# A hybrid diffusion step on one core: modulation sums queued singly behind VectorE sums of FF1, and 28 unread matmuls at the seam into FF1

## The chip, the cores and the metric

The kernel runs on one core of one Trainium2 chip. Its engines run side by side, each with a queue of its own: PE multiplies matrices into PSUM banks, VectorE (DVE) and ScalarE (ACT) do elementwise work and read the banks out, GpSimd (POOL) does a little elementwise work, and SyncE (SP) issues nearly all transfers. The metric is the device time in microseconds (us) of one execution; the median of three runs counts.

## What is computed

One inference step of one layer: a normalisation with a modulation, one input projection, a Fourier mixer and a windowed attention as two branches, a gated merge, an output projection with a residual, then a second modulated normalisation and a squared-ReLU MLP, and a last normalisation. There are 1024 latent tokens and 128 context tokens, 1024 channels wide; the MLP is 4096 wide. Cut to what matters here:

```
def modulation(cvec, w_ada, b_ada):
    m = jax.nn.silu(cvec) @ w_ada + b_ada
    return [t[:, None, :] for t in jnp.split(m, 6, axis=-1)]    # sh1, sc1, ga1, sh2, sc2, ga2

def channel_mixer(h, w_ff1, w_ff2):
    return jnp.square(jax.nn.relu(h @ w_ff1)) @ w_ff2

    x = x + ga1 * merge_branches(u_f, attn_o, g, w_fo, w_ao, w_out)
    h = rmsnorm(x, g2) * (1 + sc2) + sh2
    x = x + ga2 * channel_mixer(h, w_ff1, w_ff2)
```

The modulation vectors of both token kinds are six chunks of 1024 columns of one product with w_ada. The last, ga2, is wanted only when the MLP's result is added.

## The kernel before

**Arithmetic.** Every 32-bit operand is split into a rounded high part and the rest, the low part: ScalarE copies the high part (L145), VectorE subtracts it from the raw one (`sub`, L140). A product is three matmuls: high by high, high by low, low by high. Such a split is what stands between a weight's landing and its first use on PE; the low part is used by the third matmul.

**Stages.** Input projection, Fourier mixer, attention, branch projections, output projection (`wout_mm`, token tiles in three groups), FF1 and FF2. FF1 and FF2 work by a seven-product scheme (Strassen's) on blocks of tokens and channels. FF1 goes over 16 column pairs of w_ff1 (256 columns each). The body of a pair `p` takes seven products with 512 columns of tokens (`prod`, L1267: 12 matmuls each) and one product for the context tokens (`step_ctx`, L1311: 24 matmuls with 256 columns). The products go into PSUM banks from a pool of six (`gt`); the small ones, transposes among them, into a pool of two (`mmt`). VectorE adds banks up (`ev_p6`, `ev_p7`, `ev_c2`, `ev_p3`: L1341, L1350, L1355, L1367), ScalarE applies the squared ReLU (L1286, L1287), VectorE forms block sums for FF2's scheme (L1380 to L1389), and SP stores the blocks. VectorE also forms weight sums for the next products (`ff1_sums`, L1089 to L1092, one of which goes into the tile `SA`, which was the context tile's place before).

**The modulation's steps.** From the third chunk on the modulation is worked off in blocks of 256 columns, beside other work (`mod_blocks`, L286). A block is ten steps. Steps 0 to 7 each load 128 x 256 of w_ada over SP (L299) into one of two slots and do two VectorE operations with it, one for each token kind (L310 in step 0, L312 in the others), which add a multiple of it to an accumulator. Steps 8 and 9 transpose and sum up (L321, L322). `mod_fold`, called in the middle of the next block, ends a block with a small matmul and four additions (L268, L272). 40 steps (`MOD_LATE`), the four blocks of ga2, are left when FF1 begins. In FF1 the two slots and the accumulator lie in `zh(15, 2)`, the place of the last tile of the output projection (L1493).

**Who sets the order.** The code is traced in the order of its lines, and a planner that simulates the engines puts each engine's instructions into a queue: an instruction that is ready in its simulation may be drawn ahead of others that were traced earlier, and the earlier traced goes first among those that are ready. Between L1239 and L1492, the seam from the output projection into FF1, the order of PE, VectorE, ScalarE and GpSimd is written out by hand: `manual_schedule` keeps the listed instructions in their order, but instructions traced after it can still be put between them. `tc.issue_after(ins)` lets what is traced under it be queued on the engine of `ins` only behind `ins`; instructions on other engines, a load on SP for example, are not bound by it.

**The seam.** In this order PE does: the last parts of the output projection (`unit_end`), products 1 and 2 of the first pair with three of four token tiles (`step_p1(0, RA)`, which needs one of the six banks free; `step_p2`, which adds into the same bank after ScalarE has read it in `ev_p1`, L1296), products 6, 7, 5, 4, 3 with transposes (`fin_c`, L1165) between, then the same products for the last token tile (`RB`), the context tile's transposes, the context product and its last transposes. The context product needs `cth` and `ctl`, the high and low parts of the context tile: a ScalarE copy (L1481) and a VectorE subtraction (L1482, recorded as L140, BT<-ZR). After it the loop over pairs 1 to 15 begins (L1541).

Of the kernel before, what the change touches and what calls it, by code (L numbers as in the profile page):

```python
# [14 lines left out]
ALU = mybir.AluOpType  # L15
# [22 lines left out]
CH = 384  # L38
# [20 lines left out]
def backbone_kernel(  # L59
# [26 lines left out]
    nc = tc.nc  # L86
    uid = [0]

    def nm(s):
        uid[0] += 1  # L90
        return f"{s}_{uid[0]}"
# [32 lines left out]
    def mmt():  # L124
        return pmm.tile([P, 512], F32, tag="mm", name=nm("mm"))
# [43 lines left out]
    def mod(k, m, tok):  # L169
        return mods[:, k * 8 + m, tok : tok + 1]  # L170
# [161 lines left out]
    def mod_step(n):  # L332
        for _ in range(n):
            if msteps:
                msteps.pop(0)()

    with ExitStack() as sf:
        qa = sf.enter_context(tc.tile_pool(name="qa", bufs=6, space=PSUM))

        def bank6():  # L340
            return qa.tile([P, 512], F32, tag="x", name=nm("x"))
# [4 lines left out]
        with ExitStack() as s0:  # L346
# [6 lines left out]
            ps = mmt()  # L353
# [29 lines left out]
            for t0 in range(0, NTT, 3):  # L383
# [8 lines left out]
                for t, xt in zip(range(t0, t0 + 3), xts):  # L392
# [4 lines left out]
                    for hh in range(2):  # L397
                        ps = bank6()
# [102 lines left out]
        for o in range(0, NDFT, 1024):  # L501
            n = min(1024, NDFT - o)
# [9 lines left out]
        for gi in range(4):  # L512
# [17 lines left out]
            for s in range(4):  # L530
                r = slice(s * 512, (s + 1) * 512)
                anchor = mm3(pa, sth[:, s], stl[:, s], dhi[:, r], dlo[:, r], s == 0, s == 3)
            for s in range(2):
                r = slice(2048 + s * 256, 2304 + s * 256)
# [22 lines left out]
            e = gi % 2  # L557
# [371 lines left out]
    def gt():  # L929
        return q3.tile([P, 512], F32, tag="x", name=nm("x"))  # L930
# [27 lines left out]
    with ExitStack() as sao:  # L958
# [18 lines left out]
        for m in range(KC):  # L977
# [4 lines left out]
            for j in range(NJ):  # L982
                r = slice(j * CH, (j + 1) * CH)
# [7 lines left out]
        for m in range(KC):  # L991
            blk = load_w(w_ao, 0, KC, m * P, P)
            for j in range(NJ):
                ps = gt()
# [22 lines left out]
    def tsel(n):  # L1017
        return (tev, TE[n]) if n in TE else (tbv, TB[n])
# [61 lines left out]
    def uhi(raw):  # L1080
        h_, l_ = (wp.tile([P, D], F32R, tag=w, name=nm(w), bufs=3) for w in ("whi", "wlo"))
        nc.scalar.copy(h_, raw)
        return h_, l_
# [20 lines left out]
    def wout_mm(ps, t, h, k, w):  # L1104
        c = slice(h * HB, (h + 1) * HB)
        mh, ml = mview(t)[:, 0, k, :], mview(t)[:, 1, k, :]
        wh, wl = w
        nc.tensor.matmul(ps, mh, wh[:, 0, c], start=(k == 0), stop=False)
        nc.tensor.matmul(ps, mh, wl[:, 0, c], start=False, stop=False)
        nc.tensor.matmul(ps, ml, wh[:, 0, c], start=False, stop=(k == KC - 1))  # L1110
# [49 lines left out]
    def fin_c(t, kh):  # L1160
        tok = 0 if t < 8 else 1
        px = mmt()
        hn, yt = XS[t % 3], ys[t]
        for q in range(4):
            nc.tensor.transpose(px[:, q * P : (q + 1) * P], hn[:, (kh * 4 + q) * P : (kh * 4 + q + 1) * P], ident)  # L1165
        for q in range(4):
            k = kh * 4 + q
            src = px[:, q * P : (q + 1) * P]
            if kh == 0:
                nc.scalar.activation(yt[:, k], src, AF.Identity, bias=mod(3, k, tok), scale=s2[:, k, tok : tok + 1])  # L1170
            else:
                nc.vector.tensor_scalar(yt[:, k], src, s2[:, k, tok : tok + 1], mod(3, k, tok), ALU.mult, ALU.add)
# [74 lines left out]
    def unit_end(t, h):  # L1247
        wout_mm(b3[t, h], t, h, *last[1])

    T = {}  # L1250
    for n in (1, 2, 3, 4, 5, 6, 7):
        v, j = tsel(n)
        T[n] = [(v[:, :, j, 0, k, :], v[:, :, j, 1, k, :]) for k in range(4)]

    def wsel(p, i):
        u = wu[p]
        if i in (1, 2, 4):
            h_, l_ = u[1] if i == 1 else u[2]
            c = slice(P, 2 * P) if i == 4 else slice(0, P)
            return [(h_[:, k, c], l_[:, k, c]) for k in range(4)]  # L1260
        h_, l_ = u["u3"] if i in (5, 6) else u["u4"]
        e = {5: 0, 6: 1, 7: 0, 3: 1}[i]
        return [(h_[:, e, k], l_[:, e, k]) for k in range(4)]

    R4 = (0, 4)

    def prod(ps, p, i, r=R4, cont=False):  # L1267
        t0, tn = r
        po = ps[:, : tn * P].rearrange("p (t c) -> p t c", t=tn)
        for k, ((wh, wl), (xh, xl)) in enumerate(zip(wsel(p, i), T[i])):  # L1270
            xh, xl = xh[:, t0 : t0 + tn], xl[:, t0 : t0 + tn]
            nc.tensor.matmul(po, wh, xh, start=(k == 0 and not cont), stop=False, skip_group_check=cont)  # L1272
            nc.tensor.matmul(po, wh, xl, start=False, stop=False, skip_group_check=cont)  # L1273
            nc.tensor.matmul(po, wl, xh, start=False, stop=(k == 3), skip_group_check=cont)  # L1274
# [4 lines left out]
    def win(x, r):  # L1279
        return x[:, : r[1] * P]  # L1280

    def obuf(p, r, what):
        return place[p][what][:, r[0] * P : (r[0] + r[1]) * P]

    def relu2(v):
        nc.scalar.activation(v, v, AF.Relu)  # L1286
        nc.scalar.activation(v, v, AF.Square)  # L1287

    def step_p1(p, r=R4):
        s_ = st[p, r] = {"a": gt()}  # L1290
        prod(s_["a"], p, 1, r)

    def ev_p1(p, r=R4):
        s_ = st[p, r]
        s_["u2"] = obuf(p, r, 0)
        nc.scalar.copy(s_["u2"], win(s_["a"], r))  # L1296

    def step_p2(p, r=R4):
        prod(st[p, r]["a"], p, 2, r, cont=True)
# [38 lines left out]

    def ev_p6(p, r=R4):
        s_ = st[p, r]  # L1340
        nc.vector.tensor_tensor(s_["u2"], win(s_["b"], r), s_["u2"], ALU.add)  # L1341

    def step_p7(p, r=R4):
        st[p, r]["c"] = gt()
# [2 lines left out]
    def ev_p7(p, r=R4):  # L1347
        s_ = st[p, r]
        s_["u3"] = obuf(p, r, 2)
        nc.vector.tensor_tensor(s_["u3"], win(s_["c"], r), s_["u2"], ALU.add)  # L1350

    def ev_c2(p, r, half, keep):
        s_ = st[p, r]
        v = obuf(p, r, 3) if keep else s_["u3"]
        nc.vector.tensor_tensor(v, win(s_["d" if half else "e"], r), s_["u3"], ALU.add)  # L1355
        relu2(v)

    def step_p5(p, r=R4):
        st[p, r]["d"] = gt()
        prod(st[p, r]["d"], p, 5, r)  # L1360
# [50 lines left out]
    u2 = uhi(flat(r1))  # L1411
# [5 lines left out]
    wu[0][2] = tuple(map(k4, u2))  # L1417
    for h in range(2):
        unit_end(8, h)
    step_p1(0, RA)  # L1420
    ev_p1(0, RA)
    step_p2(0, RA)
    fin_b1(6, 2)
    u3 = uhi(zh(9, 2))
# [46 lines left out]
    step_p5(0, RB)  # L1471
    step_p6(0, RB)
    ev_p6(0, RB)
    fin_c(8, 0)
    fin_c(8, 1)
    step_p2(0, RB)
# [54 lines left out]
    def pre_prep():  # L1531
# [6 lines left out]
        load_hc(2, hc_tile("whi"))  # L1538
        load_hc(3, hc_tile("wlo"))

    for p in range(1, NPR):  # L1541
        if p == 1:
            ff1_u(p, 2)
        step_p1(p)
        ev_p1(p)
        step_p4(p)
        if p > 1:
            step_p3(p - 1)
            ev_p3(p - 1)
            del wu[p - 1]  # L1550
        ff1_sums(p)
        step_p2(p)
        ev_p2(p)
        if p + 1 < NPR:
            ff1_load(p + 1)
        else:
            pre_load()
        step_ctx(p)
        step_p6(p)
        ev_p6(p)  # L1560
        store_57(p - 1)
        step_p7(p)
        ev_p7(p)
        store_63(p - 1)
        ev_c2(p, R4, 0, True)
        store_first(p, 1)
        store_first(p, 2)
        if p + 1 < NPR:
            ff1_u(p + 1, 1)
        else:  # L1570
            pre_prep()
        step_p5(p)
        ev_c2(p, R4, 1, False)
        store_first(p, 4)
        if p + 1 < NPR:
            ff1_u(p + 1, 2)
        step_ctx2(p)
        if 1 < p < 15:
            mod_step(3)
        if p == 14:  # L1580
            mod_step(len(msteps))
            mod_fold()
            ga_rows(5, 2)
# [335 lines left out]
```

## Time and profile before

| | us |
|---|---|
| median of three runs | 1704.38 |
| lowest and highest of the three | 1703.29, 1705.64 |
| the profiled execution, its own time | 1706.87 |
| its span in the trace | 1705.1 |
| PE busy in the span | 1637.5 (96%) |
| VectorE busy | 1184.5 (69%) |
| ScalarE busy | 904.3 (53%) |

The span runs from the first to the last instruction; 1.8 us of the execution lie around it. The seam lies between 960 and 1016 us, the rest of FF1 ends near 1340, FF2 at the end of the span. A wait is put down to the one whose signal came last. "PEclk" is the clock that was granted to PE as a share of 2.4 GHz; the lower level, 1.2 GHz, is 0.50, and a value between is a mean over a stretch with both.

### The profile page before, as it was taken

The numbers are of one execution on the slowest core, as the hardware profiler recorded it, in microseconds if no ns is written. First come the engines' busy times: TensorE is split into PE (matmuls) and PEld (weight loads), VectorE is DVE, ScalarE is ACT, GpSimd is POOL, SyncE is SP. The second block draws the span as 40 slices with busy tenths as digits, with TensorE's granted clock in tenths as the row PEclk, the third lists the DMA queues.
The fourth block names the chain that finished last, engine by engine and source line by source line (L and its number), as shares of the span: only waits on it lengthen the run. The fifth ranks groups of instructions, "written<-read, shape, count | busy, mean of one in ns | idle before, by whom it ended". The sixth has DMA issues, their size and how long they took to land.

```text
span 1705.1 us, 26303 instructions
## 1 busy us (share of the span) xinstructions
PE 1637.5 (96%) x9025; PEld 1452.8 (85%) x9025; DVE 1184.5 (69%) x2408; ACT 904.3 (53%) x1826; POOL 296.1 (17%) x374
## 2 busy tenths in 40 slices
PE   6999999999999999999999879999999999999997
PEld 5799889999899999899987778888888888888886
DVE  7553247778778877778757878668666488777764
ACT  6443236766767777656446644544444354444542
POOL 3410004434434544300001500000000200000000
PEclk9999999999999999999999999999999999999999
DMA  8341491223322311279655425544444996566751
GB/s 298 112 137 64 136 245 49 78 76 80 96 69 78 94 58 50 93 243 314 190 197 176 158 87 180 178 148 149 161 143 149 291 386 216 188 195 193 249 163 62
DMA packets 204629, 265.56 MB, mean 156 GB/s; under 512 B 31992, under 2 KB 132280, under 8 KB 204496
## 3 DMA queue, kind: packets, MB, share of 16 engines
q1 hardware_dynamic: 196240, 253.92, 46.3%
q0 software_dynamic: 8256, 9.96, 2.2%
q8 instruction: 71, 1.16, 0.3%
q14 instruction: 62, 0.51, 0.1%
HBM read 195.38 MB, written 68.44 MB: 155 GB/s over the span
## 4 chain that ended last, share of the span: by engine, by line
PE 74%; DVE 8%; DMA 4%; ACT 4%; issue 3%; POOL 2%; SPq 0%; DVEq 0%; ACTq 0%; POOLq 0%
PE x L1661 6%; PE x L1662 6%; PE x L1663 6%; PE x L1272 6%; PE x L1274 6%; PE x L1273 6%; PE mm L193 3%; PE mm L194 3%; PE mm L195 3%; PE x L195 2%; PE x L194 2%; PE x L193 2%; PE ptp L748 2%; DVE pt L707 2%; PE o L759 1%
## 5 line engine op out<-in xcount | busy, mean ns | idle before, releaser
L140 DVE TENSOR_TENSOR wlo<-wraw,whi 128x1024 fp32r<-128x1024 f32 x100 | 125.7, 1260 | 84.2 <-ACT whi L145 84.0
L145 ACT CAST whi<-wraw 128x1024 fp32r<-128x1024 f32 x98 | 102.5, 1050 | 101.8 <-DMA wraw<-in_w_ff_dram 21.5
L1662 PE MATMUL x<-BR 128*128 128x512 f32 x336 | 130.7, 389 | 0.0
L1663 PE MATMUL x<-BR 128*128 128x512 f32 x336 | 130.2, 389 | 0.0
L1661 PE MATMUL x<-BR 128*128 128x512 f32 x336 | 129.0, 389 | 0.0
L729 POOL TENSOR_SCALAR pt<-pt,mx 128x512 f32<-128x512 f32 (+2 forms) x144 | 96.7, 684 | 160.5 <-DVE mx L727 144.1
L719 ACT ACTIVATE pt<-pt,mx 128x513 f32<-128x513 f32 (+2 forms) x144 | 94.7, 660 | 32.7 <-DVE mx L717 32.2
L707 DVE CUSTOM_DVE_ANT_0 pt<-s,mask,sink 128x512 f32<-128x512 f32 (+2 forms) x144 | 94.7, 673 | 21.7 <-PE ptp L748 11.9
L1634 ACT CAST BR<-aa 128x512 fp32r<-128x512 f32 x80 | 49.7, 622 | 103.4 <-PE x L1662 48.2
L140 DVE TENSOR_TENSOR pl<-ptp,ph 128x512 fp32r<-128x512 f32 (+1 forms) x136 | 86.0, 640 | 14.1 <-ACT ph L753 12.8
L305 POOL TENSOR_TENSOR macc<-macc,mprod 128x512 f32<-128x512 f32 x70 | 91.9, 1313 | 20.1 <-ACT mprod L303 20.0
L194 PE MATMUL mm<-BR,whi 128*128 128x384 f32 x272 | 92.5, 340 | 0.0
L753 ACT CAST ph<-ptp 128x512 fp32r<-128x512 f32 (+1 forms) x136 | 72.5, 546 | 32.5 <-PE ptp L748 31.2
L1272 PE MATMUL x<-BR,whi 128*128 128x512 f32 (+2 forms) x204 | 80.0, 392 | 7.4 <-ACT ZR L1296 4.8
L193 PE MATMUL mm<-BR,whi 128*128 128x384 f32 x240 | 83.9, 350 | 0.0
L195 PE MATMUL mm<-BR,wlo 128*128 128x384 f32 x240 | 82.0, 342 | 0.0
L1274 PE MATMUL x<-BR,wlo 128*128 128x512 f32 (+2 forms) x204 | 78.4, 384 | 1.9 <-DVE wlo L140 1.9
L748 PE MATMUL ptp<-ident,pt 128*128 128x128 f32 x496 | 76.1, 275 | 2.2 <-ACT qT L689 2.1
L1273 PE MATMUL x<-BR,whi 128*128 128x512 f32 (+2 forms) x204 | 78.2, 383 | 0.0
L1663 PEld LDWEIGHTS x<-BR 128*128 128x128 f32 x336 | 63.0, 188 | 13.2
L1661 PEld LDWEIGHTS x<-BR 128*128 128x128 f32 x336 | 63.1, 188 | 13.1
L1662 PEld LDWEIGHTS x<-BR 128*128 128x128 f32 x336 | 63.1, 188 | 12.9
(460 smaller groups left out, 5195.0 us busy)
## 6 DMA issues: line engine op xcount, KB each, us to landing
aa<-hr_d SPq DMA_DIRECT2D x108, 256.0 KB
ab<-in_w_ff_dram SPq DMA_DIRECT2D x108, 256.0 KB
hr_d<-ZR SPq DMA_DIRECT2D x104, 256.0 KB
wraw<-in_w_in_dram SPq DMA_DIRECT2D x40, 512.0 KB
wraw<-in_w_ff_dram SPq DMA_DIRECT2D x34, 512.0 KB
mraw<-in_w_ada_dram SPq DMA_DIRECT2D x96, 128.0 KB
wraw<-in_w_out_dram SPq DMA_DIRECT2D x24, 512.0 KB
z_d<-z SPq DMA_DIRECT2D x48, 192.0 KB
```

Source lines behind the costliest of these rows:

```text
L140: eng.tensor_tensor(dst, raw, hi.bitcast(F32), ALU.subtract)
L193: nc.tensor.matmul(out, ah, bh, start=start, stop=False)
L194: nc.tensor.matmul(out, ah, bl, start=False, stop=False)
L195: return nc.tensor.matmul(out, al, bh, start=False, stop=stop).ins
L707: nc.vector.tensor_tensor_reduce(out=pt[:, e, :n], in0=sp[:, :n], in1=mask[:, m0 : m0 + n], scale=1.0, scalar=sink8[:, h0 + e : h0 + e + 1 ...
L748: nc.tensor.transpose(pst[:, bi, e, :], pt[:, e, b * P : (b + 1) * P], ident)
L1272: nc.tensor.matmul(po, wh, xh, start=(k == 0 and not cont), stop=False, skip_group_check=cont)
L1273: nc.tensor.matmul(po, wh, xl, start=False, stop=False, skip_group_check=cont)
L1274: nc.tensor.matmul(po, wl, xh, start=False, stop=(k == 3), skip_group_check=cont)
L1661: nc.tensor.matmul(ps, xh, bh, start=start, stop=False, skip_group_check=cont)
L1662: nc.tensor.matmul(ps, xh, bl, start=False, stop=False, skip_group_check=cont)
L1663: nc.tensor.matmul(ps, xl, bh, start=False, stop=stop, skip_group_check=cont)
```

## The change

Two things are done.

1. `mod_step(3)` at the end of the bodies of pairs 2 to 14 is taken out. Instead, in the bodies of pairs 2 to 11, one step each is traced behind `ev_p6`, `ev_p7` and both `ev_c2`, under `issue_after` of that VectorE sum: four steps a pair, 40 in all. The rest of the work on ga2 (`mod_fold`, `ga_rows`) comes at the end of pair 12, before at pair 14.
2. `unread(n)` issues n matmuls of 128x128 by 128x384 into a small bank that nobody reads, with the high part of the token block `T[1][0]` as both operands. 9 are put behind `unit_end(8, ...)`, 12 behind `ev_p1(0, RA)` and 7 behind `ev_p6(0, RB)`, all within the hand-written order.

```diff
+    def unread(n):
+        ps, (a, b) = mmt(), T[1][0]
+        for _ in range(n):
+            nc.tensor.matmul(ps[:, :CH], a[:, 0], a[:, 0:3], start=True, stop=True)
+
     def ev_p6(p, r=R4):
         s_ = st[p, r]
-        nc.vector.tensor_tensor(s_["u2"], win(s_["b"], r), s_["u2"], ALU.add)
+        return nc.vector.tensor_tensor(s_["u2"], win(s_["b"], r), s_["u2"], ALU.add).ins
...
     for h in range(2):
         unit_end(8, h)
+    unread(9)
     step_p1(0, RA)
     ev_p1(0, RA)
+    unread(12)
     step_p2(0, RA)
...
     step_p6(0, RB)
     ev_p6(0, RB)
+    unread(7)
     fin_c(8, 0)
...
+    def mod_behind(p, ins):
+        if 1 < p < 12:
+            with tc.issue_after(ins):
+                mod_step(1)
+
     for p in range(1, NPR):
...
         step_p6(p)
-        ev_p6(p)
+        mod_behind(p, ev_p6(p))
         store_57(p - 1)
         step_p7(p)
-        ev_p7(p)
+        mod_behind(p, ev_p7(p))
         store_63(p - 1)
-        ev_c2(p, R4, 0, True)
+        mod_behind(p, ev_c2(p, R4, 0, True))
...
         step_p5(p)
-        ev_c2(p, R4, 1, False)
+        mod_behind(p, ev_c2(p, R4, 1, False))
         store_first(p, 4)
...
         step_ctx2(p)
-        if 1 < p < 15:
-            mod_step(3)
-        if p == 14:
+        if p == 12:
             mod_step(len(msteps))
             mod_fold()
             ga_rows(5, 2)
```

`ev_p7` and `ev_c2` return their VectorE sum in the same way.

## Rows read from the trace of the kernel before

**Rows 1.** The page, part 1: busy time, share of the span, instructions.

```profile
PE 1637.5 (96%) x9025; PEld 1452.8 (85%) x9025; DVE 1184.5 (69%) x2408; ACT 904.3 (53%) x1826; POOL 296.1 (17%) x374
```

**Rows 2.** Windows of FF1 and FF2: length; busy (instructions) of PE, PEld, DVE, ACT, POOL; PEclk, DMA, GB/s.

```profile
1016.00:1340.00 324.00, 324.00 (x1614) 274.67 (x1613) 222.67 (x343) 150.34 (x233) 5.80 (x9) 1.00 0.50 158
1340.00:1690.00 350.00, 349.45 (x1543) 288.87 (x1542) 248.87 (x427) 153.58 (x282) 4.37 (x7) 1.00 0.67 224
```

**Rows 3.** Waits of PE from 950 to 1016 us: in total, times, longest.

```profile
PE x L1272 <- ACT ZR L1296: 4.8, 1, 4.8
PE mm L1319 <- DVE BT L140: 4.2, 1, 4.2
PE x L1272 <- DVE ZR L1120: 2.5, 1, 2.5
PE x L1274 <- DVE wlo L140: 1.9, 1, 1.9
PE mm L1165 <- ACT ZR L1153: 1.7, 1, 1.7
```

**Rows 4.** Windows of 4 us over the seam, columns as in rows 2.

```profile
964.00:968.00 4.00, 1.28 (x8) 0.96 (x6) 3.90 (x6) 2.94 (x7) 3.84 (x3) 1.00 0.35 131
968.00:972.00 4.00, 1.87 (x6) 1.87 (x7) 3.56 (x10) 2.77 (x7) 0.41 (x1) 0.56 0.80 253
972.00:976.00 4.00, 4.00 (x16) 4.00 (x15) 3.13 (x4) 3.13 (x5) 0.00 (x0) 0.59 0.63 181
...
1000.00:1004.00 4.00, 0.53 (x2) 0.53 (x3) 3.19 (x7) 0.00 (x0) 0.00 (x0) 0.82 0.26 80
...
1008.00:1012.00 4.00, 3.91 (x22) 3.09 (x21) 2.21 (x6) 3.40 (x5) 0.00 (x0) 0.82 0.38 128
```

**Rows 5.** Timeline at PE's second long wait: start, length, engine, line, what [idle before].

```profile
996.03 1.36 DVE L1172 TENSOR_SCALAR ZR<-mm,s,mods 128x128 f32<-128x128 f32 x4
997.52 1.04 ACT L1481 CAST BT<-ZR 128x1024 fp32r<-128x1024 f32 x1
1000.81 1.28 DVE L312 SCALAR_TENSOR_TENSOR ZR<-ZR,siluc 128x256 f32<-128x256 f32 x3 [0.84 <-DMA ZR<-in_w_ada_dram]
1002.20 1.82 DVE L140 TENSOR_TENSOR BT<-ZR,BT 128x1024 fp32r<-128x1024 f32 x2
1003.47 0.58 PE L1319 MATMUL mm<-whi,BT 128*128 128x256 f32 x1 [4.23 <-DVE BT L140]
```

**Rows 6.** Timeline: a step's load and sum, and the last transposes of two pairs.

```profile
1009.38 0.33 SPq L299 DMA_DIRECT2D ZR<-in_w_ada_dram  x1
1011.55 0.88 DVE L312 SCALAR_TENSOR_TENSOR ZR<-ZR,siluc 128x256 f32<-128x256 f32 x2 [1.28 <-DMA ZR<-in_w_ada_dram]
...
1121.28 0.38 PE L1329 MATMUL mm<-ident,ZR 128*128 128x128 f32 x2
1143.50 0.38 PE L1329 MATMUL mm<-ident,ZR 128*128 128x128 f32 x2
```

**Rows 7.** Timeline of PE: two matmuls at full clock, two in the first dip.

```profile
964.77 0.33 PE L1273 MATMUL x<-BR,whi 128*128 128x384 f32 x1
964.95 0.34 PE L1274 MATMUL x<-BR,wlo 128*128 128x384 f32 x1
...
970.62 0.52 PE L1273 MATMUL x<-BR,whi 128*128 128x384 f32 x1
970.94 0.52 PE L1274 MATMUL x<-BR,wlo 128*128 128x384 f32 x1
```

**Rows 8.** Groups by line, VectorE, 990 to 1330 us: busy, mean ns, idle before.

```profile
L312 DVE SCALAR_TENSOR_TENSOR ZR<-ZR,siluc 128x256 f32<-128x256 f32 x56 | 25.2, 478 | 9.8 <-DMA ZR<-in_w_ada_dram 9.7
```

**Rows 9.** Windows in the attention and in FF1, columns as in rows 2.

```profile
374.00:378.00 4.00, 2.17 (x13) 1.50 (x12) 3.92 (x10) 1.94 (x5) 0.00 (x0) 0.99 0.23 54
...
1032.00:1053.00 21.00, 21.00 (x108) 17.73 (x107) 17.76 (x35) 10.05 (x16) 0.00 (x0) 1.00 0.43 138
...
1116.00:1137.00 21.00, 21.00 (x107) 17.80 (x106) 12.59 (x18) 10.20 (x17) 0.00 (x0) 1.00 0.43 145
```

## What the change does to the time: the prediction

> **What bounds the kernel now.** I read the page first: the matrix engine (PE) is busy for 96% of the span [rows 1]. Next the windows: from 1016 to 1340 us it is busy for all 324 us and from 1340 to 1690 us for 349.45 of 350 [rows 2]. So behind 1016 us, in FF1 and FF2, PE alone sets the pace, and what the stage before it ends earlier, the kernel ends earlier. Third, the waits of PE in the stretch ahead, the seam between the output projection and FF1: 4.8, 4.2, 2.5, 1.9 and 1.7 us [rows 3], 15 us in all, the largest loss near the lines that the change touches. Last, windows of 4 us over the seam, for the clock [rows 4]. In two stretches the granted clock is at its lower level, 1.2 GHz for 2.4. A row's clock gives the length: 0.56 over 4 us is 3.5 us at half, so the first dip begins at 968.5 us, and 0.59 in the next row ends it at 975.3. The second runs from 1002.6 (0.82) to 1009.4 us (0.82). Each begins inside one of the two longest idle times of PE and outlasts it.
>
> **Why PE idles in the second.** The context product needs its token tile's low part (L1482, on VectorE through L140). VectorE is free of the manual order's work at 996.03 + 1.36 = 997.4 us, and the high part is there at 997.52 + 1.04 = 998.6 [rows 5]. But the low part is taken only behind 1002.20 us. Between them stand modulation sums (L310, L312) that the planner drew forward from the second pair's body, and they also wait for their own loads: 0.84 us at 1000.81 [rows 5], and later 1.28 us at 1011.55 [rows 6], with the subtraction behind them for which PE waits 1.9 us [rows 3]. VectorE takes its queue in order here, so a sum whose row block has not landed holds what stands behind it.
>
> **The change, part 1: the sums.** They are neither removed nor added. All 40 steps left for FF1 go from three at the end of a body (pairs 2 to 14) to four in each body of pairs 2 to 11, each behind a sum that reads a PE bank. That pins VectorE's part; the loads on SP are not pinned, but with two slots only two of them can go early. None of the sums can then stand in the seam. What that frees there:
> - The gap of 4.23 us. VectorE would do the two short steps of the manual order that stand ahead (0.68 and 0.28 us) from 997.6 to 998.6, just when the high part is there; the subtraction takes about 1.2 us, so PE resumes near 999.9 in place of 1003.47 [rows 5]: 3.6 us. Lower bound 2.5, if one more 128x512 subtraction (0.7 us) and a handover slip in ahead of it.
> - The second dip. From 1003.47 to 1009.4 us PE works 5.9 us at half. Its matmuls of 384 columns start every 0.32 us in the first dip and every 0.18 us at full clock [rows 7], so 44% of the time is lost: 2.6 us. With a gap of 0.7 us left there I see no dip. Lower bound 1.3, if half of it stays.
> - The wait of 1.9 us at the first pair's low half. Taken off is the load wait of 1.28 us [rows 6]: 1.3 us; between 0 and 1.9.
>
> Sum 7.5 us, between 3.8 and 8.1.
>
> Where the sums go, they cost VectorE 2 x 478 ns a step [rows 8], 3.8 us a pair. A pair lasts 1143.50 - 1121.28 = 22.2 us on PE [rows 6]; VectorE is busy 12.59 of 21 us in a pair without sums [rows 9], 13.3 a pair. 17.1 of 22.2 us is below the bound, and at nothing I cost them: they lie beside PE's products. If that cover went, see the rival below. Queued behind a pinned step on VectorE are the next bank's sum, the block sums with their stores, and the low halves of the next pair's weights; the one who waits in the end is PE, at the next pair's first product. On SP, a load that waits for its slot stands ahead of block stores and the next weight load.
>
> **Part 2: the unread matmuls.** 28 matmuls of 384 columns, 0.18 us each at full clock [rows 7]. Nine behind the last output projection: 1.6 us in a gap of 2.5. Twelve behind the first product: 2.1 us in a gap of 4.8. Seven ahead of the context tile's transposes: 1.2 us in a gap of 1.7 [rows 3]. Each bunch is shorter than its gap, so on the path they cost 0; were the twelve run at half, 12 x 0.32 = 3.8 us is still under 4.8, and seven at half (2.2 us) would cost 0.5. Their banks are the two small ones, which were emptied before; they read only blocks that the first product reads too.
>
> They can bring only clock. The first dip meets 5.1 us of work at half (from 965.3 + 4.8 = 970.1 to 975.3) [rows 4, 7] and costs 44% of it: 2.25 us. After the change the gaps are 0.9 and 4.8 - 2.1 = 2.7 us. An idle time of 2.5 us kept the clock at 1.00 in this seam, those of 4.2 and 4.8 lost it [rows 3, 4]. By the nearest row 2.7 keeps it. Against that, in the attention stage PE loses the clock at the end of a stretch in which it was still busy for 2.17 of 4 us, though at the end only [rows 9]: long idleness is not needed there. I take 1.0, somewhat under the middle of 0 and 2.25. If all of it came, the scaling on ScalarE and the sums on VectorE, which follow PE there, would be late next.
>
> **The sum.** 7.5 + 1.0 = 8.5 us. The profiled execution took 1706.87 us, 1705.1 of span and 1.8 around it; the median is 1704.38, so that execution was 2.5 us above it and the two clock dips may be part of why. Against its own time 1706.87 - 8.5 = 1698.4; against the median 1704.38 - 8.5 = **1695.9**.
>
> **A rule to weigh.** A step's load issued at 1009.38 us fed the sum at 1011.55, so 2.2 us from issue to use [rows 6]. The Trainium skill (SBUF — State Buffer, "The DMA setup-cost knee") says that every transfer pays a fixed 2 us or so whatever its bytes; the trace agrees. The rule speaks against queueing the sums singly: with two slots, the load of a step is issued only when the step two before it is done, and each single sum may meet its own fixed cost where three in a row met it as a group. What that would do is the first rival, priced from rows.
>
> **Rivals.**
> 1. *Slower: the pinned sums hold VectorE.* If each step waits for its load at its pinned place, VectorE needs 13.3 + 3.8 + 4w a pair. It passes PE's 22.2 us from w = 1.3 us on. At w = 1.5 ten pairs cost 9 us and eat the gain; at the 2.2 us of the row they cost 10 x 3.7 = 37, less 8.5: 1733 us. For it: the load waits at 1000.81 and 1011.55. Against it: four bank sums a pair lie over several products, so a load has mostly more than 2.2 us, and a planner that counts its landing puts other ready work ahead; from 1032 to 1053 us, with sums among its work, VectorE is busy 17.76 of 21 us and PE still all 21 [rows 9]. Chance 0.06.
> 2. *About the same: the seam's queue fills with something else.* The planner that drew the sums forward may draw other ready work (the next pair's weight sums, block subtractions) into the same idle time of VectorE. Then the gap stays above 2 us, the dip comes as before, and 2.2 us (4.23 - 2) is gained: 1702 us. Against it: the next weight sums write the tile that the subtraction reads, so they cannot pass it. Chance 0.08.
> 3. *The unread matmuls do not do what they are for.* The clock falls in the first gap all the same: 1696.9 us. Or they keep it wholly: 1694.6. About even, and both stay inside the forecast's case.
>
> **How the numbers follow.** The forecast's case has 0.86, rival 2 0.08, rival 1 0.06, of which 0.04 with w far enough past 1.5 to show as slower and 0.02 near it, where it shows as no change. 0.2% is 3.4 us, about what a measurement of this kernel can tell from no change. Faster 0.86, same 0.10, slower 0.04. The range: at best 3.6 + 2.6 + 1.9 + 2.25 = 10.4 us, and 1.1 for the spread of the runs shown below their median, gives 1692.9; at worst 3.8 and nothing from the clock in the first gap, 1700.6. What lies outside, on the upper side, is the 0.14 of the rivals.
>
> **What would show it.** Right: PE's wait for the context tile's low part falls from 4.2 us to under 1.5; clock 1.00 from 996 to 1016 us of the old time; no modulation sum on VectorE ahead of pair 2's first bank sum; PE still without waits in FF1; FF1's pairs still 22.2 us. For part 2: the windows behind the twelve matmuls at 1.00, and PE's second product at 0.18 us a matmul. Wrong: new waits of PE for VectorE's low halves within pairs 2 to 11, with load waits of VectorE above 1.3 us a step; or another VectorE line where the sums stood.

## The result, and the profile after

The changed kernel takes **1697.04 us** (median of 6 runs, 1694.33 to 1698.12) beside 1704.71 us for the kernel before in the same comparison (6 runs, 1701.95 to 1706.81): a ratio of 0.9939, 95% interval 0.9925 to 0.9954. Measured once more below (e4) it came out at 0.9926 (0.9914 to 0.9938). Predicted were 1695.9 us, between 1692.9 and 1700.6. The profiled execution took 1695.32 us, 1693.5 of them span, against 1706.87 and 1705.1.

First the page's busy line and the two windows of FF1 and FF2, which answer [rows 1] and [rows 2]; the windows are moved by 10 us, as FF1 came earlier by about that. Columns of all windows: stretch, length, busy (instructions) of PE, PEld, DVE, ACT, POOL, then PEclk, DMA share, GB/s.

```profile
PE 1635.2 (97%) x9053; PEld 1450.9 (86%) x9053; DVE 1184.4 (70%) x2408; ACT 903.8 (53%) x1826; POOL 297.5 (18%) x374
...
1006.00:1330.00 324.00, 324.00 (x1614) 274.70 (x1613) 229.30 (x364) 151.56 (x237) 5.81 (x9) 1.00 0.53 167
1330.00:1680.00 350.00, 350.00 (x1547) 289.77 (x1546) 247.84 (x426) 152.60 (x279) 4.38 (x7) 1.00 0.66 218
```

28 matmuls more, and VectorE has 229.30 us of work in FF1's window where it had 222.67, as sums that stood in the seam now stand there. PE is still busy for all 324 us. The waits of PE from 945 to 1016 us answer [rows 3] (in total, times, longest):

```profile
PE x L1277 <- ACT ZR L1301: 2.8, 1, 2.8
PE x L1277 <- DVE ZR L1120: 0.9, 1, 0.9
PE mm L1324 <- DVE BT L140: 0.8, 1, 0.8
PE x L1277 <- DVE ZR L1360: 0.6, 1, 0.6
PE mm L1165 <- ACT ZR L1153: 0.4, 1, 0.4
```

The lines have moved by some five: L1277 is the old L1272, L1324 the old L1319. 4.8, 4.2, 2.5 and 1.7 us became 2.8, 0.8, 0.9 and 0.4; the wait of 1.9 us for the low half of pair 1's weights is gone. Three of these fell by what the unread matmuls fill, which is no gain by itself. The clock over the seam answers [rows 4]:

```profile
964.00:968.00 4.00, 1.21 (x8) 0.88 (x7) 3.87 (x6) 2.68 (x7) 1.90 (x2) 1.00 0.63 216
968.00:972.00 4.00, 4.00 (x16) 4.00 (x15) 3.66 (x8) 3.76 (x6) 0.00 (x0) 0.57 0.79 241
972.00:976.00 4.00, 4.00 (x28) 3.97 (x27) 2.64 (x8) 2.91 (x6) 0.00 (x0) 1.00 0.44 135
...
996.00:1000.00 4.00, 3.25 (x26) 3.04 (x26) 2.75 (x5) 1.25 (x4) 0.00 (x0) 1.00 0.57 225
1000.00:1004.00 4.00, 3.58 (x23) 2.80 (x23) 2.07 (x3) 3.84 (x6) 0.00 (x0) 1.00 0.10 37
```

The first dip to 1.2 GHz is there still, but it ends with its first row (0.57 over 4 us is 3.4 us at half), where it lasted 6.8 us before; the second is gone. Last, the timeline of VectorE and PE where [rows 5] stood:

```profile
992.84 1.36 DVE L1172 TENSOR_SCALAR ZR<-mm,s,mods 128x128 f32<-128x128 f32 x4
994.46 0.69 DVE L140 TENSOR_TENSOR ER<-ZR,ER 128x512 fp32r<-128x512 f32 x1 [0.26 <-ACT ER L1056]
995.06 0.28 DVE L1355 TENSOR_TENSOR ZR<-x,ZR 128x128 f32<-128x128 f32 x1
995.26 1.88 DVE L140 TENSOR_TENSOR BT<-ZR,BT 128x512 fp32r<-128x512 f32 x2
...
997.20 0.39 PE L1324 MATMUL mm<-whi,BT 128*128 128x256 f32 x1 [0.75 <-DVE BT L140]
```

From the normalisation (L1172) to the two subtractions it is now 2.4 us, not 6.2, and no modulation sum lies between. The row of 1.88 us holds one 128x512 subtraction for the stores and then the token tile's low part: the block subtraction that the prediction's lower bound let slip in did slip in. Counted from L1172, PE goes on 3.1 us sooner (4.4 us behind it, not 7.4).

**Where the time went.** Two points and the end make the traces comparable: A, the start of the last matmul of the last output projection, and L, the start of FF1's last transpose. Before A both kernels run the same work, yet A lies anywhere from 955.0 to 962.4 us in the fourteen traces of this case, and L to the end is 359.8 to 360.5 us in all but one. So the stretch A to L is what the change can be read from.

```profile
960.09 0.39 PE L1110 MATMUL x<-whi,BT 128*128 128x512 f32 x1
L1329 PE MATMUL mm<-ident,ZR x32: 270/272/329, 1010.1 to 1345.2; 128*128 128x128 f32 x32
```

That is the kernel before: 1345.2 - 960.1 = 385.1 us. The changed kernel:

```profile
957.64 0.39 PE L1110 MATMUL x<-whi,BT 128*128 128x512 f32 x1
L1334 PE MATMUL mm<-ident,ZR x32: 270/272/308, 1001.2 to 1333.7; 128*128 128x128 f32 x32
```

1333.7 - 957.6 = 376.1 us, 9.0 less. The other 2.5 us between the two profiled executions lie before A, where nothing was changed: the trace of before has five stretches at 1.2 GHz from 240 us to A, that of after three.

### The profile page after: what moved, and what is told of

Read it like the earlier page. It is cut to its first block, busy times and chain, and to the rows that moved or that the text cites. A ratio compares the mean times of both kernels' runs of the same rounds, so it can differ in the third digit from the quotient of the medians.

```text
span 1693.5 us, 26361 instructions
## 1 busy us (share of the span) xinstructions
PE 1635.2 (97%) x9053; PEld 1450.9 (86%) x9053; DVE 1184.4 (70%) x2408; ACT 903.8 (53%) x1826; POOL 297.5 (18%) x374
## 4 chain that ended last, share of the span: by engine, by line
PE 77%; DVE 8%; ACT 4%; issue 3%; DMA 2%; POOL 1%; SPq 0%; DVEq 0%; ACTq 0%; POOLq 0%
PE x L1674 6%; PE x L1675 6%; PE x L1673 6%; PE x L1277 6%; PE x L1279 6%; PE x L1278 6%; PE mm L193 3%; PE mm L194 3%; PE mm L195 3%; PE x L193 2%; PE x L194 2%; PE x L195 2%; PE ptp L748 2%; DVE pt L707 2%; PE o L759 1%
## 5 line engine op out<-in xcount | busy, mean ns | idle before, releaser
L140 DVE TENSOR_TENSOR pl<-ptp,ph 128x512 fp32r<-128x512 f32 (+1 forms) x136 | 86.0, 640 | 15.9 <-ACT ph L753 14.8
L1277 PE MATMUL x<-BR,whi 128*128 128x512 f32 (+2 forms) x204 | 79.6, 390 | 4.1 <-ACT ZR L1301 2.8
L303 ACT ACTIVATE mprod<-mraw,siluc 128x256 f32<-128x256 f32 x140 | 63.8, 503 | 20.6 <-POOL macc L305 19.5
L140 DVE TENSOR_TENSOR BR<-aa,BR 128x512 fp32r<-128x512 f32 x80 | 55.0, 687 | 28.3 <-ACT BR L1646 27.7
L1673 PEld LDWEIGHTS x<-BR 128*128 128x128 f32 x336 | 63.1, 188 | 13.2
```

Of the source, the lines that this page charges most:

```text
L140: eng.tensor_tensor(dst, raw, hi.bitcast(F32), ALU.subtract)
L1673: nc.tensor.matmul(ps, xh, bh, start=start, stop=False, skip_group_check=cont)
```

## The experiments

All of them in one table; the low clock is read from windows of a quarter of a microsecond between A and 1016 us (1020 in e6).

| kernel | ratio to before, 95% interval | A to L, us | at 1.2 GHz in the seam, us of the trace |
|---|---|---|---|
| before | 1 | 385.1 | 968.5-975.3, 1002.6-1009.4 |
| e8, before again | 1.0007 (0.9992-1.0021) | 386.5 | 967.3-974.5, 994.8-1008.5 |
| e1, sums alone | 0.9945 (0.9933-0.9957) | 379.2 | 962.0-965.5, 968.8-972.5, 992.8-1003.0 |
| e2, unread alone | 0.9959 (0.9944-0.9975) | 381.8 | 970.5-977.5, 1011.5-1015.0 |
| after | 0.9939 (0.9925-0.9954) | 376.1 | 968.3-972.0 |
| e4, after again | 0.9926 (0.9914-0.9938) | 374.8 | none |
| e3, 26 for 12 | 0.9941 (0.9928-0.9954) | 376.3 | 999.0-1002.8 |
| e11, sums and the seven | 0.9953 (0.9935-0.9972) | 376.9 | 966.8-973.8 |
| e12, all gaps | 0.9941 (0.9924-0.9958) | 374.8 | none |
| e6, 20 in the old gap | 1.0033 (1.0019-1.0047) | 391.2 | 965.5-972.5, 989.5-1003.3, 1013.3-1020.3 |
| e5, three in a row | 1.0000 (0.9988-1.0011) | 376.0 | 968.5-972.3 |
| e9, four in a row | 0.9935 (0.9918-0.9953) | 376.1 | 966.5-970.0 |
| e10, rows at pair 14 | 0.9947 (0.9928-0.9965) | 375.0 | none |
| e7, three each | 0.9968 (0.9954-0.9982) | 379.7 | 969.5-973.0 |

**The two parts.** The changed kernel without its 28 unread matmuls:

```diff
-    unread(9)
...
-    unread(12)
...
-    unread(7)
```

> Only part 1: the 40 modulation steps singly behind VectorE sums of pairs 2 to 11; no unread matmuls. Theory (the gain is the sums' leaving the seam): 7.5 us less than the kernel before, with PE's wait for the context tile's low part near 0.7 us, no clock dip behind it, and the first dip (about 968 to 975 us of the old time) as in the kernel before. Rival (the unread matmuls carry a good part by the clock): 5 us less or under, the second dip still there.

The kernel before with them (`unread` as in the change):

```diff
+    unread(9)
     step_p1(0, RA)
     ev_p1(0, RA)
+    unread(12)
...
     ev_p6(0, RB)
+    unread(7)
```

> Only part 2: the 28 unread matmuls, the modulation steps three at the end of pairs 2 to 14 as before. Theory by the clock alone: 1 us less than before (between 0 and 2.3), PE's wait for the context tile's low part as before at 4.2 us with its dip. But the planner's queue shifts with the seven matmuls: in VectorE's queue four modulation operations instead of seven now stand ahead of that subtraction, and one block subtraction (0.7 us) more; if this holds, the wait falls to 2 to 2.5 us and the dip may go, which gives 3 to 5.5 us less in all.

The changed kernel once more:

> The changed kernel itself beside the other three on one chip: 8 us less than the kernel before, for the sum of the two parts and for the comparison with more unread matmuls.

By the medians of this comparison (before 1707.19) the sums alone bring 8.3 us, the unread matmuls alone 7.1, both 11.9 (8 were expected). The stretch A to L says 5.9 (7.3 against e8), 3.3 (4.7) and 10.3 (11.7). By the stretch the two parts about add up, and the second is several times the 1.0 us that I gave it. Each trace shows why. In e1 PE no longer waits for the token tile at all, and yet the clock falls, at 992.8 us (windows of e1):

```profile
988.00:992.00 4.00, 2.31 (x21) 2.16 (x20) 2.77 (x10) 1.98 (x4) 0.00 (x0) 1.00 0.00 0
992.00:996.00 4.00, 3.97 (x23) 3.73 (x21) 2.17 (x6) 2.98 (x9) 0.00 (x0) 0.60 0.26 72
996.00:1000.00 4.00, 4.00 (x21) 4.00 (x20) 2.41 (x4) 2.28 (x4) 0.00 (x0) 0.50 0.00 0
1000.00:1004.00 4.00, 4.00 (x24) 4.00 (x24) 1.90 (x5) 1.24 (x4) 0.00 (x0) 0.62 0.66 262
...
991.74 1.09 PE L1165 MATMUL mm<-ident,ZR 128*128 128x128 f32 x8 [1.70 <-ACT ZR L1153]
```

It falls behind an idle time of 1.7 us in the first window, PE's wait ahead of the context tile's transposes, and PE then works at 1.2 GHz for ten microseconds. So taking the sums' gap away does not keep the clock: the low stretch comes earlier, behind that wait, and is longer. In e2 the wait is filled and the long dip at 1002.6 is gone, with one of 3.5 us at 1011.5 in its place, at the end of another wait; but its gain isn't the clock's alone, for with the unread matmuls the planner also queued four instructions of sums ahead of the token tile in place of seven, and PE's wait there is 1.7 us instead of 4.2; the sums that were left stood ahead of pair 1's low half, for which it waits 2.7 instead of 1.9, and there the clock fell.

**Is the trace of before typical?** The kernel before, unchanged:

> The kernel before, unchanged, for a second trace of its seam. Theory: the waits of PE from 950 to 1016 us (4.8, 4.2, 2.5, 1.9, 1.7) come out the same within 0.3 us, as they hang on the queues, and both dips of the clock come again, so the stretch from the last matmul of the last output projection to the last transposes of FF1 is 385 us again. Rival: the dips differ from one execution to the next, as they do between the two traces of the changed kernel (one dip of 3.75 us in the seam in one, none in the other); then the stretch differs by 1.5 us or more, and what the unread matmuls are worth can't be read from one trace.

```profile
PE x L1272 <- ACT ZR L1296: 4.8, 1, 4.8
PE x L1272 <- DVE ZR L1120: 2.5, 1, 2.5
PE mm L1165 <- ACT ZR L1153: 1.7, 1, 1.7
PE x L1274 <- DVE wlo L140: 1.7, 1, 1.7
PE mm L1319 <- DVE BT L140: 0.9, 1, 0.9
```

The waits at the same places, except one: 0.9 us where [rows 3] had 4.2. Here the clock fell at 994.8 us, so that PE came later to the token tile and waited less. VectorE's timeline in e8 shows why that cost so little (A to L 386.5 against 385.1, with the low clock half as long again):

```profile
995.14 1.36 DVE L1172 TENSOR_SCALAR ZR<-mm,s,mods 128x128 f32<-128x128 f32 x4
996.81 0.62 DVE L310 TENSOR_SCALAR ZR<-ZR,siluc 128x256 f32<-128x256 f32 x2 [0.31 <-DMA ZR<-in_w_ada_dram]
...
999.60 1.37 DVE L312 SCALAR_TENSOR_TENSOR ZR<-ZR,siluc 128x256 f32<-128x256 f32 x3 [0.78 <-DMA ZR<-in_w_ada_dram]
...
1001.08 1.82 DVE L140 TENSOR_TENSOR BT<-ZR,BT 128x1024 fp32r<-128x1024 f32 x2
```

From L1172 to the subtractions it is 5.9 us, 6.2 in the other trace [rows 5]. In the kernel before, VectorE's queue with its sums and their load waits sets when PE goes on, and whether PE reaches that point early and idles or late at half clock is nearly the same. The gap and a low clock ahead of it are two faces of one delay: the gap is worth 4.2 us only where the clock has held until then. Low clock behind the gap is there in both traces, some 6 us of it (to 1008.5 us in e8, to 1009.4 in the other).

**Which bunch keeps the clock.** The changed kernel with the seven alone:

```diff
-    unread(9)
...
-    unread(12)
...
     unread(7)
```

> The changed kernel with the seven unread matmuls ahead of the context tile's transposes alone; the nine and the twelve are left out. In all four traces without unread matmuls the clock is low for 6.8 us or more between 989 and 1009 us (or on to 1003), begun 1 to 3 us behind the idle time of 1.7 us that the seven fill. Theory: the seven alone keep the clock there: at most 4 us of low clock from 985 to 1016, and the time 2 to 3.5 us under that of the sums alone; the first dip stays at 7 us. Rival (the two bunches ahead of it set the state, by keeping the first dip short): low clock of 6 us or more behind the seven, and the time of the sums alone.

```profile
988.00:992.00 4.00, 3.56 (x28) 3.24 (x28) 2.77 (x10) 1.98 (x4) 0.00 (x0) 1.00 0.02 4
992.00:996.00 4.00, 3.97 (x36) 3.74 (x35) 2.40 (x7) 3.94 (x12) 0.00 (x0) 1.00 0.24 68
996.00:1000.00 4.00, 3.06 (x24) 2.72 (x24) 3.97 (x8) 1.82 (x4) 0.00 (x0) 1.00 0.32 131
1000.00:1004.00 4.00, 3.68 (x29) 3.18 (x27) 0.94 (x2) 3.15 (x6) 0.00 (x0) 1.00 0.35 131
```

The same four windows as of e1, all at 1.00, with the first dip at 7 us as in the kernel before. A to L is 2.3 us shorter than in e1. From A to the context product VectorE's queue is the same in both but for two pairs of neighbours that changed places, so a new order of that queue is hardly the reason. The times don't tell the two apart (0.9953 and 0.9945, with overlapping intervals), so the gain of the seven stands on the traces: in all four traces without the seven the clock is low for 6.8 us or more between 989 and 1009.5 us; in the ten with them, for 3.8 us in one and not at all in nine (e2's dip at 1011.5 lies behind that stretch). In three of the four it fell in the idle time of 1.7 us or at most 2.1 us behind it. The trace of before kept it there for 8.9 us more and lost it in the gap of 4.2; whether that gap would cost the clock with the seven in place no run shows, since in e2 the gap was 1.7 us.

**More of them.** 26 in place of the twelve, and then all gaps filled:

```diff
-    unread(12)
+    unread(26)
```

> The changed kernel with 26 unread matmuls instead of twelve in the longest gap: 26 x 0.175 = 4.5 us in a gap of 5.0 us. Theory (the clock falls for idleness there): the granted clock stays at 1.00 from 960 to 980 us and PE's second product runs at 0.175 us a matmul throughout, 1.0 to 1.6 us less than the changed kernel. Rival (the clock is not what the gap costs, or the chain on ScalarE and VectorE is late next): no change. If the last unread matmuls run into the second product's start: 0.3 us more.

```diff
-    unread(9)
+    unread(13)
...
-    unread(12)
+    unread(26)
...
-    unread(7)
+    unread(9)
...
+    unread(4)
     step_ctx(0)
```

> The changed kernel with its idle times in the seam filled further: 13, 26 and 9 unread matmuls in place of 9, 12 and 7, and 4 ahead of the first context product. Waits of PE in the seam in the changed kernel: 2.8, 0.9, 0.8, 0.4 and three under 0.4 besides 0.6. Theory: they end in work, the waits fall under 2 us in all, no low clock from 955 to 1016 us, and the stretch from the last output projection's last matmul to FF1's last transposes is at its length without a dip, 374.8 us (376.1 with one); the time is 0 to 1.5 us under the changed kernel's. Rival (idle time is not what the clock goes by, as in the run with 26, where it fell behind a wait of 0.8 us): a dip of 3.75 us or more all the same, no gain, or a loss of up to 1.5 us where a bunch outlasts its gap.

With 26 the first dip was gone and another of 3.8 us came behind a wait of 0.8 us; A to L stayed at 376.3 and the time wasn't better. With all gaps filled PE's waits sum to under 2 us, the clock never falls, and the stretch is 374.8 us: what the changed kernel itself reaches in the executions without a dip (e4 374.8, e10 375.0). So one dip is worth 1.3 us here, and there is nothing more to fill.

**The unread matmuls in the wrong gap.** The kernel before, with 20 (`unread` as in the change) where PE waited 4.2 us:

```diff
+    unread(20)
     step_ctx(0)
```

> The kernel before, its sums still in the seam, with 20 unread matmuls (20 x 0.18 = 3.5 us) right ahead of the first context product, in the idle time of 4.2 us there; none elsewhere. Theory: the clock falls because PE idles there, and the sums' queue sets how long it idles. So the wait stays (unread work and rest of the wait together about 4.2 us), the windows behind it show 1.00 in place of 0.82 and lower, and the run is 1.3 to 2.6 us shorter than before by that dip alone; the first dip, near 970 us, is as before. Rival (the clock falls in this seam whatever fills that one gap): low clock behind it all the same, and no gain, or a loss if the 20 run at half clock, 20 x 0.32 = 6.4 us against 4.2.

```profile
984.00:988.00 4.00, 4.00 (x36) 4.00 (x35) 3.18 (x7) 1.74 (x4) 0.00 (x0) 1.00 0.00 0
988.00:992.00 4.00, 2.27 (x15) 2.13 (x14) 1.90 (x8) 2.96 (x7) 0.00 (x0) 0.69 0.02 4
...
999.10 1.82 DVE L140 TENSOR_TENSOR BT<-ZR,BT 128x1024 fp32r<-128x1024 f32 x2
...
999.68 5.29 PE L1270 MATMUL mm<-BR 128*128 128x384 f32 x20
```

The rival held, with the loss. The clock had fallen ten microseconds earlier, at 989.5, in the idle time of 1.7 us, so PE came late and hardly any gap was left: the token tile's low part was done at 1000.9 us, and the 20 ran until 1004.8, to 1003.3 at half. The stretch is 6.1 us longer than in the trace of before, 4.7 than in e8; behind it PE waits 3.0 us for pair 1's low half, and the clock falls once more. Filling this gap was of no use, filling a shorter one ahead of it was.

**Single or in a row.** The changed kernel with three steps in a row at the body's end, pinned behind the pair's last sum, in pairs 2 to 14 (the other three calls of `mod_behind` go as well):

```diff
-        mod_behind(p, ev_c2(p, R4, 1, False))
+        last_sum = ev_c2(p, R4, 1, False)
...
-        if p == 12:
+        if 1 < p < 15:
+            with tc.issue_after(last_sum):
+                mod_step(3)
+        if p == 14:
```

> The changed kernel, but the sums leave the seam in another way: three steps in a row at the end of the bodies of pairs 2 to 14 as before, pinned behind that pair's last sum of a bank instead of one behind each of four. Theory: what counts is that none of them stands in the seam. Then PE's wait for the context tile's low part is 0.8 us as in the changed kernel (4.2 before), seam and FF1 together stay 9 to 10 us shorter than before, and the time stays within 2 us of the changed kernel. A group takes VectorE 3 x 0.96 = 2.9 us, and its third load is issued only when the first step is done, so about 1.2 us of load wait a pair: 13.3 + 2.9 + 1.2 = 17.4 of 22.2 us a pair, still under PE. Rival (the single queueing is worth something by itself): VectorE's waits for these loads in FF1, 0.8 us in the changed kernel and 9 us before, come back to 9 us or more and reach PE: waits of PE in pairs 2 to 14, 0 in the changed kernel, of 0.3 to 1 us each, 4 us or more in all.

In the seam it did what the theory said: the same waits as after, A to L 376.0, and no wait of PE in FF1. Yet the whole gain was lost behind L, by a place that neither side had named (PE's waits from 1016 to 1690 us; a window of that stretch, then its like in the changed kernel):

```profile
PE mm L1671 <- DMA whi<-hc_d: 5.7, 1, 5.7
PE x L1671 <- DMA BR<-hs_d: 2.2, 1, 2.2
...
1322.57 0.99 SPq L936 DMA_DIRECT2D ga_d<-mods  x2
...
1324.00:1328.00 4.00, 4.00 (x25) 3.55 (x24) 2.68 (x4) 1.84 (x4) 2.85 (x4) 1.00 2.34 169
1328.00:1332.00 4.00, 4.00 (x20) 3.30 (x19) 1.66 (x3) 0.00 (x0) 0.00 (x0) 1.00 1.45 25
```

```profile
1324.00:1328.00 4.00, 4.00 (x26) 3.55 (x25) 2.21 (x4) 1.85 (x5) 2.85 (x4) 1.00 1.02 284
1328.00:1332.00 4.00, 4.00 (x19) 3.32 (x18) 1.57 (x3) 0.00 (x0) 0.00 (x0) 1.00 1.14 383
```

GpSimd issues FF2's first loads at the same time in both (1314.5 to 1334.5 us), but in e5 they move 25 GB/s where they moved 383. Between stands the store of the folded modulation rows, 1322.6 us, 11 us ahead of L; it writes 2048 numbers, each to a place of its own, and the DMA share is higher behind it (2.34) than in any other such window from 1256 to 1356 us, while little arrives. PE then waits 7.9 us, the clock falls at 1340.7 and stays at 1.2 GHz until 1351.0 us; L to the end is 371.1 us and not 359.8. The Trainium skill (DMA: Bandwidth & Descriptors, "Rules for kernel authors") says that a transfer without a contiguous last dimension becomes one descriptor per element; the rows fit that, though no run here shows the descriptors. The store is late here because the last steps are pinned to pairs 13 and 14, and the fold comes behind them. In the kernel before the same store went out at 1323.3 us, 22 us ahead of its L, and PE did not wait for these loads. Its windows there (before):

```profile
1324.00:1328.00 4.00, 4.00 (x20) 3.29 (x18) 1.89 (x3) 2.08 (x5) 1.10 (x2) 1.00 1.12 46
1328.00:1332.00 4.00, 4.00 (x19) 3.33 (x18) 1.83 (x3) 2.13 (x3) 0.53 (x1) 1.00 1.08 23
```

The changed kernel, where the store goes out at 1268.2 us, shows the same from 1268 to 1276 us (1.02 at 108 GB/s, 1.10 at 27). So in all three traces some 8 us follow the store in which the DMA share is above 1.0 and little is moved; e5 is the one in which they begin 10 us ahead of L. Two runs test it:

```diff
-    def mod_behind(p, ins):
-        if 1 < p < 12:
+    def mod_behind(p, ins, n=0):
+        if n and 1 < p < 12:
             with tc.issue_after(ins):
-                mod_step(1)
+                mod_step(n)
...
-        mod_behind(p, ev_c2(p, R4, 1, False))
+        last_sum = ev_c2(p, R4, 1, False)
...
+        mod_behind(p, last_sum, 4)
         if p == 12:
```

With n left at 0 the other three calls do nothing.

> The three-in-a-row kernel lost 11 us at FF2's entry (PE waits of 5.7 and 2.2 us for loads, and low clock behind them), not in FF1: there the store of the modulation rows, which that kernel issues at 1322.6 us, lies upon FF2's first loads. This run keeps the grouping and takes that away: four steps in a row at the end of the bodies of pairs 2 to 11, pinned behind the pair's last sum, and the fold with the store of its rows at pair 12 as in the changed kernel. Theory: single or grouped makes no difference; no waits at FF2's entry, PE without waits of over 0.5 us in FF1, the time within 2 us of the changed kernel (some 11 us under before). VectorE: 13.3 + 3.8 + some 2 us of load wait = 19 of 22.2 us a pair. Rival: single queueing is worth something by itself; then VectorE's load waits come to 1 us a pair or more and PE waits for it in FF1, 3 us or more in all.

```diff
-        if p == 12:
+        if p == 14:
             mod_step(len(msteps))
             mod_fold()
             ga_rows(5, 2)
```

> The changed kernel with one line changed: the fold of the last sums and the store of their rows stand at the end of pair 14's body, as before, and not of pair 12's. Theory: the store then lies upon FF2's first loads as in the three-in-a-row kernel: it is issued some 10 to 20 us ahead of FF2's first matmul, a window there shows a DMA share over 1.2 at under 100 GB/s, PE waits 3 to 9 us at FF2's entry, and the time is 4 to 11 us above the changed kernel. Rival (the planner draws fold and store forward, as it did in the kernel before, where the store was issued 22 us ahead of FF1's last transposes and PE waited only 0.4 us at FF2's entry): no wait over 0.5 us and the time of the changed kernel.

e9 is as fast as the changed kernel, and no PE wait is left behind 1016 us. So the single queueing is not what brings the gain. It is not without an effect on VectorE: its load waits in FF1 are 14.8 us in e9 and 0.8 us in the changed kernel (VectorE's waits from 1016 to 1345 us, e9 first),

```profile
DVE ZR L312 <- DMA ZR<-in_w_ada_dram: 14.8, 10, 3.6
```

```profile
DVE ZR L312 <- DMA ZR<-in_w_ada_dram: 0.8, 1, 0.8
```

but PE doesn't see them: VectorE has the room. e10 went against my expectation: with the steps themselves still done by pair 11, the planner drew fold and store forward, the store went out at 1311.4 us, 22 us ahead of L, and nothing waited for it. So moving the fold from pair 14 to 12 cost and gained nothing by itself that these runs resolve. What e5 lost came from steps pinned into the last two pairs; that the scattered store is the carrier rests on the windows above and on the two runs without it there; no run took the store alone away.

**How far VectorE's room goes.** Three steps behind each sum in the third to sixth pair:

```diff
-        if 1 < p < 12:
+        if 1 < p < 6:
             with tc.issue_after(ins):
-                mod_step(1)
+                mod_step(3)
```

> The changed kernel with three steps behind each of the four sums of a bank in the third to sixth pair, in place of one in the third to twelfth. It is the size at which rival 1 of the prediction should decide: VectorE needs 13.3 + 12 x 0.96 = 24.8 us a pair, without any load wait, against PE's 22.2. Theory: PE waits for VectorE in pairs 3 to 5; 3 x 2.6 = 8 us lost against the changed kernel if the loads never hold VectorE, so about the time of before; with 0.8 us of load wait a step (12 x 0.8 = 9.6 a pair) some 35 us lost, 1730 us. Rival (VectorE has room that its busy time doesn't show, since later pairs catch up and banks lie between): PE without waits in FF1 and the time of the changed kernel within 2 us.

```profile
PE mm L268 <- DVE red L322: 3.2, 1, 3.2
PE x L1279 <- DVE wlo L140: 0.5, 1, 0.5
...
DVE ZR L312 <- DMA ZR<-in_w_ada_dram: 12.6, 8, 2.9
```

PE waits in FF1 at last, but for 3.7 us in all, 3.2 of them for a fold's sums (L268); A to L is 3.6 us longer than after, not 8, still less 35. The steps ran from 1042 to 1130 us, four pairs where 40 steps at twelve a pair take 3.3, so they slipped behind the places that I had counted; and one step in five, the transposing and summing up, has no load. Rival 1 exists, at three times the load that the change puts on VectorE, and then weakly.

## Why the prediction was right, and where its working was not

- **The bound.** Right: PE sets the pace from FF1 on. L to the end is the same in every kernel but e5, and what the seam ends earlier the kernel ends earlier.
- **The gap of 4.23 us.** Right in itself: 0.75 us is left, 0.7 was forecast. With the slipped subtraction of the lower bound PE goes on 3.1 us sooner, between the 2.5 and 3.6 stated.
- **The second dip, 2.6 us.** This step failed. I hung it on the sums' gap because it began there. In e1 the gap is gone and the clock is low for longer (10.3 us for 6.8), behind the wait of 1.7 us; in e11 the seven unread matmuls take that away. So the sums alone did not bring the 2.6 us; they came with part 2, where e11 gives 2.3.
- **The wait of 1.9 us for pair 1's low half.** Gone whole: the upper bound, where I took 1.3.
- **The sums' part, 7.5 us.** Measured in e1: 5.9 us against the trace of before, 7.3 against e8. PE's waits in the seam fall from 15.9 to 8.6 us in all, 7.3 less, the gap (4.2 to nothing, as PE comes late there) and the last wait (1.9) above all; 3.4 us more of low clock take some of it back. Inside the bounds of 3.8 to 8.1.
- **The unread matmuls, 1.0 us (0 to 2.25).** Mis-sized: 3.1 us (379.2 to 376.1) to 4.4 (to 374.8), of which the seven bring 2.3 and the other two bunches 0.8 to 2.1; the medians of e1 and e4 give 3.6. The sign that I had named, clock 1.00 behind the twelve, failed in the profiled execution (0.57) and came in e4. I gave the twelve and the first dip all the attention and the seven none, as their gap was the shortest.
- **The sum, 8.5 us.** Measured 7.7 and, in the comparison of e4, 11.9 by the medians, 9.0 and 10.3 by the stretch in two traces: right, with one term too large and the other too small by about as much. That the two errors nearly cancel was luck. The profiled execution came out at 1695.3 where the sum against its own time gave 1698.4; 2.5 of these 3.1 us lie ahead of the seam.
- **The clock in the first gap (rival 3).** About even, as forecast: behind an idle time of 2.8 us the changed kernel lost it in one trace and kept it in the other; with e5, e7, e9 and e10, where this code is the same, it is four against two. The row that I leaned on, an idle time of 2.5 us that kept the clock, was no guide: e1 lost it behind one of 2.4.
- **Rival 1.** Its load wait was 0.8 us for all the steps together, where it needed 1.3 us for each. By the Trainium skill's rule (SBUF — State Buffer, "The DMA setup-cost knee") I had weighed that single sums might each meet the fixed cost of a transfer. The runs went the other way: spread out, a step's load has landed when its turn comes; four in a row, pinned, waited 14.8 us in ten places.
- **Rival 2.** It did not come in the changed kernel; e2, where the queue was still free, showed the planner does rearrange that stretch at small cause.
- **What the prediction left out.** The fold and the store of its rows moved from pair 14 to pair 12 with the steps, so that the store goes out at 1268.2 and not at 1323.3 us, further ahead of FF2's first loads. I costed neither. e10 shows that it was worth nothing here; e5, that the same store placed badly takes the whole gain.

## What to carry to other kernels

Where one engine idles and its clock falls, look for the idle time ahead of the one where the dip begins: here the bunch in the shortest of the three filled gaps brought most, and 20 matmuls in one of 4.2 us made the kernel slower. A wait for another engine's queue and a low clock ahead of that wait are one delay and may be counted once. When work is pinned, follow everything at its end too (here a fold and a scattered store): it arrives where it has never been before.

## What the hardware showed beside that

- An idle time of 1.7 us was followed by 10 to 14 us at 1.2 GHz in three traces, most of it with PE busy (e1 10.3, e8 13.8, e6 13.8 us); in the trace of before the clock held for 8.9 us behind it. Idle times of 2.8 us were followed by none in two traces of six.
- The same program has its dips in different places in different executions; the start of the seam (A) moved by 7 us over the fourteen traces, all with the same work ahead of it, which is nearly the size of the effect. The medians did not resolve 2 us; a stretch cut out between two instructions of the trace did.
- Two stores of 1024 scattered numbers each were followed by some 8 us with a DMA share above 1.0, in the second half of which 23 to 27 GB/s were moved in all (before, after and e5).
